# A buffer exchange in the first stage and new orders for the first and the last stage of a hybrid trunk kernel

## The chip, the cores and the metric

The kernel runs on one core of a Trainium2 chip. The metric is the device time of one execution in microseconds (us); lower is better. The profile calls the engines PE (TensorE, the matrix products; PEld is its weight load), DVE (VectorE), ACT (ScalarE), POOL (GpSimd) and SP (SyncE, which here only issues DMAs). [...]

## The reference

Two layers run over 512 latent tokens and 256 context tokens of width 1024. Each sub-layer is normed, shifted and scaled by a modulation of the conditioning vector, and its output is normed, gated and added to the residual stream:

```python
sh1, sc1, gt1, sh2, sc2, gt2 = ada_terms(c[:, None, :], w_mod[layer], b_mod[layer])
a = modulate(rms_norm(h, g_mix_pre[layer]), sh1, sc1)
...
y, yc = hybrid_mixer(a, ac, ...)      # layer 0: gated DeltaNet heads and attention heads
y = conformer_conv(a, *conf)          # layer 1
h = h + gt1 * rms_norm(y, g_mix_post[layer])
f = swiglu_ffn(modulate(rms_norm(h, g_ffn_pre[layer]), sh2, sc2), w_ffn_in[layer], w_ffn_out[layer])
h = h + gt2 * rms_norm(f, g_ffn_post[layer])
```

The context tokens enter layer 0 only, where they feed keys, values and the states of the DeltaNet heads. `conformer_conv` is a projection with a gate, a depthwise convolution over 31 tokens, a layer norm and a projection. `swiglu_ffn` is a gated product through 2816 hidden channels. Everything is float32.

## The kernel before, in words

A float32 product is made of three products of split operands: high by high, low by high and high by low, where `whi` is the rounded weight, `wlo` the remainder, and `ah`, `al` the same for activations. So nearly every product comes as three matmuls in turn, and every weight block of 128 x 1024 (512 KB, tile `wraw`) has first to be cast (`whi`, L564) and subtracted (`wlo`, L573).

The work goes in four stages. In each, operations are entered in a list by `op(...)`, with the engines that may do them and a cost on each, and class `Plan` then places them one at a time. Where an operation can go to two engines, the plan picks one. What is placed next is the operation with the smallest

```python
key = start - self.weight * lead, i
```

where `lead` is the length of the path behind the operation plus a number from a table `BIAS`, one per name of operation. The four tables are constants of the file. The plan runs when the kernel is built; on the chip each engine runs its own fixed list and waits by semaphore for data and buffers. A buffer pool is a `slot` in the plan (`take`, `rel`) and a tile with as many `bufs` in the code.

**First stage (`plan_inputs`, table `BIAS0`, 0 to 57 us).** Six token tiles of 128 x 1024 (four latent, two context; tile `xt`, three buffers) are loaded (`ld_x`, L351), squared and summed on ACT (`x_sq`, L355), get their root on DVE and POOL (L358, L180), are scaled in place on ACT or DVE (`x_norm`, L365 or L367), turned on PE in two halves of four transposes (`x_turn`, L374) and copied out of PSUM on ACT or DVE (`x_copy`, L314). Beside this sixteen modulation blocks of 512 KB (`mraw`, six buffers, `ld_m`, L404) are multiplied by the conditioning vector on PE (`mods`, L411). Two blocks make one group j of 128 channels: their rows are copied, turned on PE (`turn`, L426) and made into columns (L430, L431), and with these `mod` (L446, L448) shifts and scales the turned tokens, `a_high` rounds and `a_low` (L454) subtracts. The key and value products (`kv`, L297 to L299) follow, group by group. The PSUM banks of the turned tokens are those of the key and value products, so the latter begin when all six tiles are turned and copied out.

**Heads, and delta rule with attention (57 to 217 us and 217 to 392 us).** These two stages have tables of their own.

**Last stage (`BIAS2`, 392 to 1376 us).** The output projection, the first FFN, the conformer and the second FFN. `out_proj` makes token tiles t by halves n of the channels: matmuls into `ps_y` (L1760 to L1762), sum of squares on ACT (L1781), gate on DVE (`yg`, L1785), then root on POOL, residual on DVE (`hres`, L1810). The next sub-layer then norms (`xm`, L570), turns on PE (`ps_a`, L1832), and splits into `ah` and `al`. The gate, shift and scale rows of later sub-layers are made on DVE by 80 products with blocks `wada` of 512 KB (L1627), spread over the stage. The conformer convolves as a product in a transformed domain: its activations `ul`/`uh` go through PE (`ps_ft`), DVE and POOL form `spa`, `spb`, these are split (`sph`, `spl`, L573), and PE brings them back (`ps_y`, L2285 to L2287).

SP issues every load in the order that the plan wrote; an issue that waits for a buffer holds up all behind it.

Of the kernel before, what the change touches and what calls it, by code (L numbers as in the profile page):

```python
# [151 lines left out]
def kernel(ctx: ExitStack, tc: tile.TileContext, I: dict, out: bass.AP, dbg=None):  # L152
# [149 lines left out]
    with ExitStack() as st:  # L302
# [15 lines left out]
        def plan_inputs(op):  # L318
            last = {}
# [26 lines left out]
            def row_tile(t):  # L346
                s = {}

                def ld_x():
                    s["x"] = sp.tile([P, D], F32, tag="xt", name="xt", bufs=3)  # L350
                    SP.dma_start(s["x"], I["xs"][t * P : (t + 1) * P, :] if t < 4 else I["ctx"][(t - 4) * P : (t - 3) * P, :])  # L351

                def x_sq():
# [2201 lines left out]
```

## Time and profile before

| | us |
|---|---|
| median of 3 runs | 1379.72 (1378.24 to 1382.68) |
| the profiled execution, its own time | 1377.72 |
| its span, first to last instruction | 1375.9 |
| PE busy in the span | 1326.7 |
| mean granted clock of PE | 0.992 |

The profiled execution is 1.8 us longer than its span. A row of a timeline names an engine, a line of the kernel and what was written from what; the bracket behind it is the time for which the engine stood idle before it, and what released it. Rows that run back to back are drawn together with their count. The products of `mods` and `turn` are recorded as two matmuls each where the program has one, so eight records are one modulation block; eight transposes are one token tile.

### The profile page before, as it was taken

What the parts mean: (1) busy time and instruction counts of PE and PEld (TensorE: products, weight loads), DVE (VectorE), ACT (ScalarE), POOL (GpSimd) and SP (SyncE); (2) the same over time, 40 slices, a digit from 0 to 9 for tenths busy, and PEclk for the clock granted to TensorE, in tenths of its full rate; (3) what the DMA queues carried; (4) which work ended last, traced back from release to release, by engine and by line L of the source; (5) the groups of instructions that cost most, each with busy time, mean ns of one, the idle gap of its engine ahead of it and who ended that gap; (6) DMA issues with size and microseconds to landing.
All of it is one profiled execution on the core that took longest, in us unless ns stands there. A gap on an engine that the chain in (4) does not pass through costs nothing.

```text
span 1375.9 us, 19258 instructions
## 1 busy us (share of the span) xinstructions
PE 1326.7 (96%) x7343; PEld 1116.3 (81%) x7343; DVE 857.8 (62%) x1625; ACT 453.4 (33%) x983; POOL 256.7 (19%) x347
## 2 busy tenths in 40 slices
PE   5999898999999999999999999999999999999998
PEld 4888797898877888888887878887798888888886
DVE  3588897888888666565667476649663334243223
ACT  6656534877524301111000142114342223222221
POOL 2668563411002300000000011323040000000000
PEclk9999998999999999999999999999999999999999
DMA  8445636641157464545557333201113223233231
GB/s 320 136 147 165 157 116 148 218 143 55 38 203 262 158 200 150 185 160 177 184 202 256 117 103 103 73 28 62 61 65 120 92 92 110 74 122 108 93 105 64
DMA packets 105900, 184.76 MB, mean 134 GB/s; under 512 B 33776, under 2 KB 50496, under 8 KB 105808
## 3 DMA queue, kind: packets, MB, share of 16 engines
q1 hardware_dynamic: 105808, 183.53, 41.3%
q8 instruction: 58, 0.95, 0.3%
q14 instruction: 34, 0.28, 0.1%
HBM read 172.45 MB, written 11.06 MB: 133 GB/s over the span
## 4 chain that ended last, share of the span: by engine, by line
PE 74%; DVE 12%; DMA 7%; issue 2%; ACT 2%; POOL 2%; SPq 1%; DVEq 0%; POOLq 0%; ACTq 0%
PE ps_in L204 12%; PE ps_in L206 12%; PE ps_in L205 12%; PE ps_y L1760 5%; PE ps_y L1762 5%; PE ps_y L1761 5%; DMA wada<-in_wmB 3%; PE ps_in L2114 2%; PE ps_in L2112 2%; PE ps_in L2113 2%; DVE wlo L573 2%; PE ps_pt L1271 2%; DVE cv L653 2%; DVE wada L1627 1%; PE ps_pv L1293 1%
## 5 line engine op out<-in xcount | busy, mean ns | idle before, releaser
L205 PE MATMUL ps_in<-al,whi 128*128 128x512 f32 (+1 forms) x768 | 285.7, 372 | 1.6 <-POOL al L573 1.6
L206 PE MATMUL ps_in<-ah,wlo 128*128 128x512 f32 (+1 forms) x768 | 285.5, 372 | 0.8 <-DVE wlo L573 0.8
L204 PE MATMUL ps_in<-ah,whi 128*128 128x512 f32 (+1 forms) x768 | 285.9, 372 | 0.0
L573 DVE TENSOR_TENSOR wlo<-wraw,whi 128x1024 fp32r<-128x1024 f32 x162 | 204.7, 1265 | 116.4 <-ACT whi L564 109.2
L204 PEld LDWEIGHTS ps_in<-ah,whi 128*128 128x128 f32 x768 | 144.6, 188 | 28.1 <-issue 2.3
L205 PEld LDWEIGHTS ps_in<-al,whi 128*128 128x128 f32 x768 | 144.6, 188 | 27.3 <-POOL al L573 2.3
L206 PEld LDWEIGHTS ps_in<-ah,wlo 128*128 128x128 f32 x768 | 144.6, 188 | 26.7 <-DVE wlo L573 2.1
L180 POOL TENSOR_TENSOR rr<-rr,mhalf 128x1 f32<-128x1 f32 x28 | 17.4, 624 | 790.6 <-DVE rr L1799 765.0
L564 DVE CAST whi<-wraw 128x1024 fp32r<-128x1024 f32 x93 | 64.8, 697 | 158.0 <-PE ps_in L205 108.6
L1760 PE MATMUL ps_y<-whi,hh 128*128 128x512 f32 x352 | 138.0, 392 | 1.8 <-DVE yg L1785 1.8
L1762 PE MATMUL ps_y<-wlo,hh 128*128 128x512 f32 x352 | 137.7, 391 | 0.0
L1761 PE MATMUL ps_y<-whi,hl 128*128 128x512 f32 x352 | 137.6, 391 | 0.0
L1965 ACT ACTIVATE sg<-ps_in 128x512 f32<-128x512 f32 x44 | 26.3, 598 | 302.9 <-PE ps_in L206 302.6
L564 ACT CAST whi<-wraw 128x1024 fp32r<-128x1024 f32 x69 | 72.3, 1049 | 122.7 <-PE ps_y L1761 70.5
L1627 DVE CUSTOM_DVE_ANT_0 wada<-wada,csrow 128x1024 f32<-128x1024 f32 x80 | 97.3, 1231 | 19.7 <-DMA wada<-in_wmB 19.4
L1760 PEld LDWEIGHTS ps_y<-whi,hh 128*128 128x128 f32 x352 | 66.2, 188 | 16.5 <-DVE yg L1785 2.2
L1762 PEld LDWEIGHTS ps_y<-wlo,hh 128*128 128x128 f32 x352 | 66.2, 188 | 14.5
L1761 PEld LDWEIGHTS ps_y<-whi,hl 128*128 128x128 f32 x352 | 66.2, 188 | 14.3
L1781 ACT ACTIVATE junk<-ps_y 128x512 bf16<-128x512 f32 x32 | 19.1, 598 | 137.5 <-PE ps_y L1762 121.0
L1968 DVE TENSOR_TENSOR sg<-sg,ps_in 128x512 f32<-128x512 f32 x44 | 29.1, 682 | 45.5 <-PE ps_in L206 45.5
L653 DVE SCALAR_TENSOR_TENSOR cv<-ps_in,convw,cv 128x510 f32<-128x510 f32 (+3 forms) x80 | 48.9, 639 | 2.6 <-ACT cv L568 1.1
L2112 PE MATMUL ps_in<-whi,ah 128*128 128x512 f32 x128 | 50.0, 391 | 0.0
(390 smaller groups left out, 2584.0 us busy)
## 6 DMA issues: line engine op xcount, KB each, us to landing
wraw<-in_wfin SPq DMA_DIRECT2D x88, 512.0 KB
wada<-in_wmB SPq DMA_DIRECT2D x80, 512.0 KB
wraw<-in_wfout SPq DMA_DIRECT2D x44, 512.0 KB
mraw<-in_wmA SPq DMA_DIRECT2D x16, 512.0 KB
wraw<-in_wcin SPq DMA_DIRECT2D x16, 512.0 KB
wraw<-in_wqkv SPq DMA_DIRECT2D x12, 512.0 KB
wraw<-in_wcout SPq DMA_DIRECT2D x8, 512.0 KB
rw<-grow SPq DMA_DIRECT2D x8, 384.0 KB
```

Of the source, the lines that this page charges most:

```text
L204: E.matmul(ps, wh, xh, start=start, stop=False)
L205: E.matmul(ps, wh, xl, start=False, stop=False)
L206: E.matmul(ps, wl, xh, start=False, stop=stop)
L564: {"ACT": S.copy, "DVE": V.tensor_copy, "Pool": G.tensor_copy}[e](dst, src)
L573: {"DVE": V, "Pool": G}[e].tensor_tensor(dst, a, b, o)
L653: V.scalar_tensor_tensor(s["cv"][:, o], s["ps"][:, i], convw[:, ft, j : j + 1], s["cv"][:, o], op0=ALU.mult, op1=ALU.add)
L1627: V.tensor_tensor_reduce(s["raw"], s["raw"], csrow[0], 1.0, 0.0, ALU.mult, ALU.add, accs[:, part, j : j + 1])
L1760: E.matmul(acc[t], ah[:, ts_], wh[:, o], start=i == 0 and j == 0, stop=False)
L1761: E.matmul(acc[t], al[:, ts_], wh[:, o], start=False, stop=False)
L1762: E.matmul(acc[t], ah[:, ts_], wl[:, o], start=False, stop=end)
L1968: V.tensor_tensor(s["g"], s["g"], pss[1]["ps"], ALU.mult)
L2112: E.matmul(acc[t], k["h"][:, tk], wh[:, o], start=False, stop=False)
```

## The change

Two tables get new numbers: `BIAS0` and `BIAS2`. The buffers of the first stage are exchanged: five token tiles instead of three, four modulation blocks instead of six. In the plan's reckoning the first token load is given a longer way to its first user. The tables of the other two stages stay, and their PE, DVE, ACT and POOL orders are the same as before.

```diff
-BIAS0, TW0 = {'a_high': 75700, 'a_low': 206192, 'c_silu': -16514,
...
+BIAS0, TW0 = {'a_high': 4187, 'a_low': 281059, 'c_silu': 232311,
...
-BIAS2, TW2 = {'a_dot': -8768, 'a_dot1': -7091, 'a_dot3': -1746,
...
+BIAS2, TW2 = {'a_dot': -6282, 'a_dot1': -450, 'a_dot3': 2428,
...
-                    s["x"] = sp.tile([P, D], F32, tag="xt", name="xt", bufs=3)
+                    s["x"] = sp.tile([P, D], F32, tag="xt", name="xt", bufs=5)
...
-                a = last["x"] = op({"SP": 1.47}, ld_x, seq=after("x"), lat=DLAT, take=("xt",))
+                a = last["x"] = op({"SP": 1.47}, ld_x, seq=after("x"), lat=DLAT if "x" in last else DLAT + 2, take=("xt",))
...
-                        w["raw"] = sp.tile([P, 1024], F32, tag="mraw", name="mraw", bufs=6)
+                        w["raw"] = sp.tile([P, 1024], F32, tag="mraw", name="mraw", bufs=4)
...
-        plan = Plan({"a": 6, "r": 2, "xt": 3, "mraw": 6, "wraw": 2, "w": 4, "rows": 2, "a32": 2, "wkr": 2}, BIAS0, TW0, SCALE0)
+        plan = Plan({"a": 6, "r": 2, "xt": 5, "mraw": 4, "wraw": 2, "w": 4, "rows": 2, "a32": 2, "wkr": 2}, BIAS0, TW0, SCALE0)
```

The first place is PE from the first instruction to the first key and value product. Before (`x24` are three token tiles of eight transposes, `x4` of L411 one modulation block, L426 the turn of one group):

```order
L374 MATMUL ps_xt<-masks,xt 128x128 x24
L411 MATMUL ps_mod<-mraw,cz 32x256 x12
L426 MATMUL ps_mod<-quart,rows 128x2 x2
L374 MATMUL ps_xt<-masks,xt 128x128 x12
L411 MATMUL ps_mod<-mraw,cz 32x256 x4
L374 MATMUL ps_xt<-masks,xt 128x128 x4
L426 MATMUL ps_mod<-quart,rows 128x2 x2
L374 MATMUL ps_xt<-masks,xt 128x128 x8
L411 MATMUL ps_mod<-mraw,cz 32x256 x8
```

After, the same engine from the first instruction (behind these rows come the sixth token tile in two halves, a block behind each half, and a third turn, and then the first L297):

```order
L374 MATMUL ps_xt<-masks,xt 128x128 x8
L411 MATMUL ps_mod<-mraw,cz 32x256 x4
L374 MATMUL ps_xt<-masks,xt 128x128 x8
L411 MATMUL ps_mod<-mraw,cz 32x256 x4
L374 MATMUL ps_xt<-masks,xt 128x128 x8
L411 MATMUL ps_mod<-mraw,cz 32x256 x4
L374 MATMUL ps_xt<-masks,xt 128x128 x8
L426 MATMUL ps_mod<-quart,rows 128x2 x2
L411 MATMUL ps_mod<-mraw,cz 32x256 x4
L374 MATMUL ps_xt<-masks,xt 128x128 x8
L426 MATMUL ps_mod<-quart,rows 128x2 x2
L411 MATMUL ps_mod<-mraw,cz 32x256 x4
```

Blocks and turns now stand between single token tiles, and before the first key and value product there are seven blocks and three turns where there were six and two. On SP the first loads are now four latent tiles and one context tile, then three modulation blocks, then the last context tile; on ACT all six `x_norm` stand (L365), between the squares, and of the twelve `x_copy` eleven are on DVE.

The second place is DVE where the first half of the first FFN's output projection ends (`yg` takes it out of PSUM, the rows L1627 are products with `wada` blocks). Before:

```order
L573 TENSOR_TENSOR wlo<-wraw,whi 128x1024
L1627 ISA wada,accs<-wada,csrow 128x1024
L1627 ISA accs 128x1
L1627 ISA wada,accs<-wada,csrow 128x1024
L1627 ISA accs 128x1
L564 CAST whi<-wraw 128x1024
L573 TENSOR_TENSOR wlo<-wraw,whi 128x1024
L1627 ISA wada,accs<-wada,csrow 128x1024
L1627 ISA accs 128x1
L1785 TENSOR_TENSOR yg<-ps_y,gm 128x512 x3
```

After:

```order
L573 TENSOR_TENSOR wlo<-wraw,whi 128x1024
L564 CAST whi<-wraw 128x1024
L573 TENSOR_TENSOR wlo<-wraw,whi 128x1024
L564 CAST whi<-wraw 128x1024
L573 TENSOR_TENSOR wlo<-wraw,whi 128x1024
L1785 TENSOR_TENSOR yg<-ps_y,gm 128x512 x3
L564 CAST whi<-wraw 128x1024
```

The `wada` products of this part now stand further ahead, in the FFN's first half, and `yg` follows a weight split directly.

The third place is POOL in the last part of the conformer (`wlo` is the split of a whole weight block, `spl` that of the transformed activations). Before:

```order
L573 TENSOR_TENSOR ul<-csg,uh 128x256
L573 TENSOR_TENSOR spa<-spa,spd 128x512
L573 TENSOR_TENSOR spb<-spb,spc 128x512
L573 TENSOR_TENSOR wlo<-wraw,whi 128x1024 x2
L573 TENSOR_TENSOR spl<-spa,sph 128x512
L180 TENSOR_TENSOR mv<-mv,mhalf 128x1 x2
L573 TENSOR_TENSOR ul<-csg,uh 128x256
L573 TENSOR_TENSOR wlo<-wraw,whi 128x1024
L180 TENSOR_TENSOR mv<-mv,mhalf 128x1 x2
```

After:

```order
L573 TENSOR_TENSOR ul<-csg,uh 128x256
L573 TENSOR_TENSOR wlo<-wraw,whi 128x1024
L573 TENSOR_TENSOR spa<-spa,spd 128x512
L573 TENSOR_TENSOR spb<-spb,spc 128x512
L573 TENSOR_TENSOR wlo<-wraw,whi 128x1024 x2
L573 TENSOR_TENSOR ul<-csg,uh 128x256 x7
L573 TENSOR_TENSOR wlo<-wraw,whi 128x1024
L573 TENSOR_TENSOR ul<-csg,uh 128x256
L180 TENSOR_TENSOR mv<-mv,mhalf 128x1 x2
L573 TENSOR_TENSOR wlo<-wraw,whi 128x1024 x2
```

`spl` is gone from POOL, all twelve are on DVE now, and POOL has three `wlo` more in this piece; from the last tiles of the first FFN's output projection (820 us) to the end it has eight where it had five. In the out-projection around 430 us the transposes of the second token tile (L1832) stand six matmuls later on PE than before, and DVE has two `wada` products fewer ahead of the tile's `xm`.

## Rows read from the trace of the kernel before

**Rows 1.** Waits of PE, 0 to 57 us: total us, times, longest us.

```profile
PE ps_xt L374 <- DVE ssq_in L358: 12.4, 2, 10.9
```

**Rows 2.** Timeline of PE, 10 to 29 us: start, length, engine, line, work, [idle <-releaser].

```profile
10.92 4.63 PE L374 MATMUL ps_xt<-masks,xt 128*128 128x128 f32 x24 [10.92 <-DVE ssq_in L358]
15.48 1.50 PE L411 MATMUL ps_mod<-mraw,cz 128*32 128x256 f32 x24
17.10 0.61 PE L426 MATMUL ps_mod<-quart,rows 128*128 128x2 f32 x4
...
28.88 0.39 PE L297 MATMUL ps_kv<-wkhi,aL 128*128 128x272 f32 x1
```

**Rows 3.** Stretches: length, busy of PE, PEld, DVE, ACT, POOL, granted clock, DMA share, GB/s.

```profile
12.00:14.00 2.00, 2.00 (x12) 2.00 (x11) 1.48 (x4) 0.81 (x2) 0.55 (x1) 1.00 0.43 125
18.00:20.00 2.00, 0.55 (x5) 0.58 (x6) 0.98 (x2) 0.88 (x1) 0.51 (x1) 1.00 0.96 309
22.00:24.00 2.00, 1.98 (x12) 0.91 (x12) 1.29 (x2) 1.94 (x5) 0.92 (x2) 0.50 1.01 413
28.88:56.80 27.92, 27.92 (x253) 23.21 (x250) 10.56 (x30) 19.63 (x38) 15.30 (x15) 1.00 0.59 210
229.70:243.30 13.60, 12.60 (x92) 10.50 (x93) 7.74 (x20) 3.84 (x16) 2.86 (x10) 0.50 0.46 128
```

**Rows 4.** Timeline of the SP queue, 2 to 16 us.

```profile
2.59 1.38 SPq L351 DMA_DIRECT2D xt<-in_xs  x3
...
12.92 0.33 SPq L351 DMA_DIRECT2D xt<-in_xs  x1
```

**Rows 5.** Groups, 0 to 57 us: line, work, count, busy us, mean ns, idle.

```profile
L454 POOL TENSOR_TENSOR aL<-a,aL 128x512 fp32r<-128x512 f32 x8 | 10.4, 1296 | 11.0 <-ACT aL L314 10.9
...
L355 ACT ACTIVATE sq<-xt 128x1024 bf16<-128x1024 f32 x6 | 6.3, 1057 | 7.8 <-DMA xt<-in_xs 6.0 <-DMA xt<-in_ctx 1.6
...
L367 DVE TENSOR_SCALAR xt<-xt,ssq_in 128x1024 f32<-128x1024 f32 x6 | 4.5, 752 | 2.4 <-POOL ssq_in L180 2.3
```

**Rows 6.** Timeline of ACT, 8 to 10 and 21 to 25 us.

```profile
8.11 1.06 ACT L355 ACTIVATE sq<-xt 128x1024 bf16<-128x1024 f32 x1 [5.54 <-DMA xt<-in_xs]
9.07 0.19 ACT L355 ACTIVATION_READ_ACCUMULATOR sq<-xt 128x1 f32 x1
...
21.49 0.57 ACT L314 COPY xnT<-ps_xt 128x512 f32<-128x512 f32 x1
...
22.94 0.62 ACT L314 CAST aL<-a 128x512 fp32r<-128x512 f32 x1
...
23.94 1.10 ACT L338 CAST wkhi<-wkr 128x1088 fp32r<-128x1088 f32 x1
```

**Rows 7.** Waits of PE, 392 to 1376 us.

```profile
PE ps_a L1832 <- DVE xm L570: 3.1, 3, 1.7
...
PE ps_y L1760 <- DVE yg L1785: 1.8, 1, 1.8
...
PE ps_y L2286 <- DVE spl L573: 1.4, 1, 1.4
PE ps_y L1760 <- DVE ah L564: 1.2, 1, 1.2
```

**Rows 8.** Timeline of PE at 430 us.

```profile
430.69 1.06 PE L1832 MATMUL ps_a<-masks,xm 128*128 128x128 f32 x8 [1.12 <-DVE xm L570]
```

**Rows 9.** Timeline of DVE, 753 to 757 us.

```profile
753.58 1.23 DVE L1627 CUSTOM_DVE_ANT_0 wada<-wada,csrow 128x1024 f32<-128x1024 f32 x1
...
754.74 1.88 DVE L1785 TENSOR_TENSOR yg<-ps_y,gm 128x512 f32<-128x512 f32 x3
```

**Rows 10.** Timeline of DVE, 930 to 934 us.

```profile
930.22 0.68 DVE L573 TENSOR_TENSOR spl<-spa,sph 128x512 fp32r<-128x512 f32 x1
...
931.27 2.78 DVE L573 TENSOR_TENSOR spl<-spa,sph 128x512 fp32r<-128x512 f32 x1
```

**Rows 11.** Timeline of POOL, 931 us.

```profile
930.97 2.53 POOL L573 TENSOR_TENSOR wlo<-wraw,whi 128x1024 fp32r<-128x1024 f32 x1 [0.78 <-ACT whi L564]
```

More of the change, by code (lines that the diff above doesn't have):

```diff
@@ L132 @@
 XORD = (0, 1, 2, 3, 4, 5)
-BIAS0, TW0 = {'a_high': 75700, 'a_low': 206192, 'c_silu': -16514, 'c_tanh': 107271, 'col': 14441, 'e_ba': 122312, 'e_k': -53254, 'e_v': 50987, 'kv': -3858, 'ld_c': 46560, 'ld_k': -23712, 'ld_late': 35862, 'ld_m': -23721, 'ld_w': -44965, 'ld_x': -23461, 'mod': -8614, 'mods': 34406, 'quarters': 63428, 'rows': -16997, 'turn': -2462, 'w_high': 99939, 'w_low': 28294, 'x_copy': -10948, 'x_eps': 223488, 'x_norm': 166269, 'x_root': -3445, 'x_sq': 28280, 'x_turn': -3427, ('a_high', 'ACT'): 107926, ('a_high', 'DVE'): -198559, ('a_low', 'DVE'): 25709, ('a_low', 'Pool'): 56700, ('e_ba', 'ACT'): 44340, ('e_ba', 'DVE'): 44577, ('e_k', 'ACT'): 58673, ('e_k', 'DVE'): 49378, ('e_v', 'ACT'): -173612, ('e_v', 'DVE'): -10933, ('mod', 'ACT'): 3301, ('mod', 'DVE'): -9021, ('rows', 'ACT'): -15795, ('rows', 'DVE'): 40653, ('w_low', 'DVE'): 128023, ('w_low', 'Pool'): 46775, ('x_copy', 'ACT'): 9199, ('x_copy', 'DVE'): 8932, ('x_norm', 'ACT'): -81145, ('x_norm', 'DVE'): 61895}, 0.000200
+BIAS0, TW0 = {'a_high': 4187, 'a_low': 281059, 'c_silu': 232311, 'c_tanh': 40826, 'col': 135122, 'e_ba': 126776, 'e_k': 155419, 'e_v': 228586, 'kv': -6027, 'ld_c': 85019, 'ld_k': -25467, 'ld_late': 33477, 'ld_m': -25475, 'ld_w': 11636, 'ld_x': -23852, 'mod': -40306, 'mods': 118753, 'quarters': 54203, 'rows': 81455, 'turn': -4629, 'w_high': 15179, 'w_low': -332635, 'x_copy': 85335, 'x_eps': 366451, 'x_norm': 27921, 'x_root': 1752, 'x_sq': 107381, 'x_turn': -5686, ('a_high', 'ACT'): 92650, ('a_high', 'DVE'): -546573, ('a_low', 'DVE'): 58817, ('a_low', 'Pool'): 146574, ('e_ba', 'ACT'): 62505, ('e_ba', 'DVE'): 63100, ('e_k', 'ACT'): 129098, ('e_k', 'DVE'): 46060, ('e_v', 'ACT'): -269350, ('e_v', 'DVE'): 12404, ('mod', 'ACT'): 25634, ('mod', 'DVE'): 33866, ('rows', 'ACT'): -100952, ('rows', 'DVE'): 250644, ('w_low', 'DVE'): 430085, ('w_low', 'Pool'): -182664, ('x_copy', 'ACT'): 3255, ('x_copy', 'DVE'): 8749, ('x_norm', 'ACT'): 180579, ('x_norm', 'DVE'): -196162}, 0.000200
@@ new lines @@
+BIAS2, TW2 = {'a_dot': -6282, 'a_dot1': -450, 'a_dot3': 2428, 'a_end': 45182, 'a_end1': 27038, 'a_end3': 6873, 'b_high2': -58633, 'b_low2': 29028, 'b_sel2': -13825, 'c_comb2': -25178, 'c_high2': 125362, 'c_low2': -4724, 'c_open2': 18314, 'c_prod2': 58271, 'c_sig2': 68975, 'c_stat2': 28892, 'c_tok2': 136341, 'c_u2': 463, 'dft2': 54461, 'dft_q2': 52342, 'f_hi2': 33389, 'f_high1': 16934, 'f_high3': -62569, 'f_lo2': 12893, 'f_low1': 33751, 'f_low3': 41869, 'f_mult1': 134913, 'f_mult3': 9578, 'f_silu1': 45895, 'f_silu3': 63658, 'g_out': 23829, 'g_out1': -20936, 'g_out3': -28337, 'idft2': -172, 'idft_q2': -1472, 'ld_a': 73451, 'ld_a1': -8751, 'ld_a3': 209823, 'ld_b2': 41420, 'ld_f2': 71483, 'ld_g0': 27200, 'ld_g1': 93269, 'ld_g2': -9319, 'ld_g3': -29463, 'ld_h0': 7435, 'ld_s2': 1589, 'ld_w0': 18625, 'ld_w1': -2304, 'ld_w2': 69622, 'ld_w3': -14691, 'm_eps1': -5278, 'm_eps2': 8332, 'm_eps3': 7671, 'm_root1': 21497, 'm_root2': -11897, 'm_root3': 70059, 'm_sq1': -13259, 'm_sq2': -7014, 'm_sq3': 119678, 'm_x1': 11013, 'm_x2': -29310, 'm_x3': -5834, 'mm_in1': -279, 'mm_in3': 94, 'mm_q2': -1314, 'n_aggr2': 14267, 'n_root2': -722, 'n_x2': 108371, 'p_high1': 95748, 'p_high2': 34429, 'p_high3': -10939, 'p_low1': 30784, 'p_low2': 90184, 'p_low3': 15409, 'put1': -15738, 'put2': -2282, 'put3': 68953, 'q_comb2': -4970, 'q_cross2': 5014, 'q_hi2': 59756, 'q_lo2': 6027, 'q_prod2': 1128, 'reopen0': -80626, 'reopen1': -27164, 'reopen2': -32064, 's_mm2': -425, 's_put2': 72757, 'sp_hi2': 86991, 'sp_lo2': 59371, 'turn1': 11545, 'turn2': -271, 'turn3': 372, 'w_high0': 37508, 'w_high1': -159, 'w_high2': 2700, 'w_high3': 12123, 'w_low0': -32633, 'w_low1': 6514, 'w_low2': -5308, 'w_low3': 2305, 'y0': 871, 'y1': -4195, 'y2': -1584, 'y3': -118928, 'y_gate0': -2595, 'y_gate1': 30797, 'y_gate2': 1623, 'y_gate3': 15631, 'y_out3': -5278, 'y_res0': 8425, 'y_res1': -2763, 'y_res2': -1630, 'y_res3': -54137, 'y_root0': -8057, 'y_root1': 69924, 'y_root2': 41319, 'y_root3': -20071, 'y_sq0': -11883, 'y_sq1': -6243, 'y_sq2': 132, 'y_sq3': -36116, 'y_sum0': 37525, 'y_sum1': 52651, 'y_sum2': 23826, 'y_sum3': 97639, ('c_comb2', 'DVE'): -93901, ('c_comb2', 'Pool'): 34957, ('c_high2', 'ACT'): -116703, ('c_high2', 'DVE'): -2104, ('c_low2', 'DVE'): -14694, ('c_low2', 'Pool'): -13796, ('c_tok2', 'ACT'): 164820, ('c_tok2', 'DVE'): -24244, ('f_hi2', 'ACT'): -81770, ('f_hi2', 'DVE'): -51553, ('f_high1', 'ACT'): 84539, ('f_high1', 'DVE'): -71245, ('f_high3', 'ACT'): 45880, ('f_high3', 'DVE'): 44098, ('f_lo2', 'DVE'): 16554, ('f_lo2', 'Pool'): 21600, ('m_x1', 'ACT'): -50339, ('m_x1', 'DVE'): 54699, ('m_x2', 'ACT'): 51663, ('m_x2', 'DVE'): 72006, ('m_x3', 'ACT'): -12006, ('m_x3', 'DVE'): 6349, ('p_high1', 'ACT'): 18569, ('p_high1', 'DVE'): 9342, ('p_high2', 'ACT'): -40127, ('p_high2', 'DVE'): 5353, ('p_high3', 'ACT'): 14702, ('p_high3', 'DVE'): -137240, ('p_low1', 'DVE'): -34721, ('p_low1', 'Pool'): 12765, ('p_low2', 'DVE'): 120412, ('p_low2', 'Pool'): 69480, ('p_low3', 'DVE'): -57419, ('p_low3', 'Pool'): 62538, ('put1', 'ACT'): -7630, ('put1', 'DVE'): -74386, ('put2', 'ACT'): -7911, ('put2', 'DVE'): -6482, ('put3', 'ACT'): 27983, ('put3', 'DVE'): 70173, ('q_hi2', 'ACT'): 92517, ('q_hi2', 'DVE'): 80834, ('q_lo2', 'DVE'): -2487, ('q_lo2', 'Pool'): -29951, ('s_put2', 'ACT'): 112996, ('s_put2', 'DVE'): 37610, ('sp_hi2', 'ACT'): -24786, ('sp_hi2', 'DVE'): -7550, ('sp_lo2', 'DVE'): 103951, ('sp_lo2', 'Pool'): -77334, ('w_high0', 'ACT'): -88042, ('w_high0', 'DVE'): -33645, ('w_high1', 'ACT'): -105124, ('w_high1', 'DVE'): 4279, ('w_high2', 'ACT'): -10100, ('w_high2', 'DVE'): -8635, ('w_high3', 'ACT'): -2195, ('w_high3', 'DVE'): -7036, ('w_low0', 'DVE'): 172190, ('w_low0', 'Pool'): -126486, ('w_low2', 'DVE'): -614, ('w_low2', 'Pool'): -19785}, 0.000200
```

1 line of the change is left out of this document (removed).

## The prediction

> **What bounds the kernel now.** I read the waits of PE first, stage by stage, since PE is busy for 1326.7 of the 1375.9 us of the span. In the first stage the waits are long and few: 12.4 us for the roots of the token tiles, 10.9 of them before the first transpose [rows 1]. The timeline of PE shows the rest of the picture: three tiles turned in one run from 10.92 us, three modulation blocks, a turn, and then a thin stretch until the first key and value product at 28.88 [rows 2]. From there to 56.80 PE is busy for 27.92 of 27.92 us [rows 3], so what is gained before 28.88, or taken out of what lies behind it, moves the end of the stage by as much. The stretches tell why the middle is thin: DMA moves 125 GB/s in 12 to 14 us against 413 in 22 to 24, PE is busy for 0.55 of 2 us in 18 to 20, and afterwards its granted clock is 0.50 [rows 3]. SP shows the cause: three token loads go out at 2.59, and the fourth only at 12.92, when a token buffer is free [rows 4].
>
> In the last stage PE seldom waits. Its list of waits [rows 7] names DVE nearly throughout, and I followed three of them back: the one at 430.69 (1.12 us) [rows 8], the 1.8 us for `yg`, and the 1.4 us for `spl`. The two middle stages keep their orders and only shift.
>
> **First stage.** Before, the start of the key and value products hung on PE and the late loads. After, five token loads go out at once, so I expect the DMA gap to close and ACT to become what is late, because it gets the six scalings as well as the six squares. One square is 1.06 us on ACT with 0.19 to read its sum [rows 6]. A scaling of this size on ACT does not stand in the trace; from below I bound it by the same on DVE, 0.75, from above by two copies of half a tile on ACT, 0.57 each, 1.14 [rows 5, 6]. I take 1.06, the square of the same shape on the same engine. Six of each, 6 x (1.06 + 0.19 + 1.06) = 13.9 us, start at 8.11 as now and end at 22.0. The last scaling waits for its own root: before, the first turn starts at 10.92, which is 1.0 us more than 9.17 (end of the first square) plus 0.75 (scaling on DVE), and that is DVE and POOL. So 23.0. Then ACT casts the key weights, 1.10, and copies, shifts and rounds the first group, which before took from 21.49 to 23.56, 2.1 us; POOL subtracts, 1.30 [rows 5, 6]. Sum 27.5, and with 0.3 of handing over 27.8. DVE takes eleven of twelve copies out of PSUM, but it gives up six scalings and is busy for only about 1.3 of 2 us here [rows 3], so it is not late. The start comes 1.1 us earlier.
>
> Behind the start one block and one turn fewer are left, since seven and three are done where it was six and two: 1.50 / 3 = 0.50 and 0.61 [rows 2], another 1.1 us. The first stage so gives 2.2 us. From the good side: if ACT waits for nothing and the scalings cost 0.75, the start is at 24.6 by the same sum, bounded by PE itself, and I stop at 4 us in all. From the bad side: the four modulation buffers. A freed buffer is wanted again three blocks later. In the key and value part PE takes ten blocks in 27.92 us, 2.8 each, so 8.4 us; before it, seven blocks in some 14 us, so 6 us. A load takes up to 5.5 us (issued at 2.59, the first square at 8.11) [rows 4, 6]. That covers it by 0.5 us in the worse part; if a load takes 1 us longer there, three blocks are late by about that much each and the start is at 30 or so, which turns the gain into a loss of 1 to 2 us. So the term is -2.2, with ends -4 and +2.
>
> The low clock at 22 to 24 us goes with the thin stretch ahead of it. In the new order 14.6 us of PE work (six tiles at 4.63 / 3 = 1.54, seven blocks, three turns) lie between about 12 and 27.8, evenly, so I expect the clock to stay up. It pays little, since ACT is what is late then.
>
> **Last stage.** At 430.69 the transposes wait 1.12 us for `xm` [rows 8]. They now stand six matmuls later (six of 0.23 us, 1.4) and DVE has two `wada` products of 1.23 [rows 9] fewer ahead. The wait goes: -1.1, ends -1.1 and 0. What is late next is the same tile's split, and its matmuls stand behind the other out-projection work.
>
> At 755 PE waits 1.8 us for the banks that `yg` empties [rows 7]. DVE reads `wada` at 753.58 for 1.23 us and comes to `yg` at 754.74 [rows 9]. After, no such product stands in front of it; `yg` goes right behind a weight split. The wait goes: -1.8, ends -1.8 and 0. The 80 `wada` products are as many as before; they move into the first half of the FFN, where four for two blocks of matmuls leave DVE under three quarters busy by my count, so I cost them at nothing. If that cover fails, a weight is split late by one product, 1.2 us.
>
> The other waits of the list (`al` near 450, `xm` at 825, `spl` and `ah` in the conformer) I cost at no change. PE's order is rewritten around them, and each is a matter of tenths in a list that I can walk only with durations of the old order. Bounds: the 1.4 and 1.2 us of `spl` and `ah` and the rest of `xm`, 2.0, gone, -4.6; or the loss that the third rival prices.
>
> Sum: -2.2 - 1.1 - 1.8 = -5.1 us, from 1377.72 of the profiled execution to 1372.6. The median of the runs lies 2.0 us above the profiled execution, and I carry that over: 1374.6.
>
> **The rivals.** First, **the waits come back**. The tail's waits are set by small slips of DVE and POOL; one taken at 430 or 755 may be paid at the next `xm` or `al`. For it: at 430 a wait of the same kind follows within 25 us. Against it: at 755 the cause is a single instruction in the wrong place. Then only the first stage remains: 1379.72 - 2.2 = 1377.5.
>
> Second, **more waits go**: the conformer is rewritten most, and with 4.6 us there at stake, half of it gives 1372.3, all of it 1370.0.
>
> Third, on the other side, **POOL blocks DVE**. The subtraction `spl` of 128x512 takes 0.68 us on DVE, and 2.78 when it starts at 931.27, while POOL subtracts a whole weight from 930.97 on for 2.53 us [rows 10, 11]; both end within 0.6 us of each other. That is 2.1 us lost, of which 1.4 reach PE [rows 7]. From 820 us to the end POOL has five such `wlo` before, and three of PE's waits there (1.7, 1.4 and 1.2, together 4.3 us) follow one; after, it has eight, and all `spl` are on DVE. If all eight hit at 1.45 us, the waits are 11.6, 7.3 more than now: 1374.6 + 7.3 = 1381.9; if each costs PE the whole 2.1, 16.8, 12.5 more: 1387.1. It outweighs the 5.1 us of gains once four hits come on top of the three of before (4 x 1.45 = 5.8). Against it: the order may put the eight where DVE reads PSUM, and only three of five hit now.
>
> [...]
>
> Fourth, **the clock**. From 229.70 to 243.30 PE runs at 0.50 and is busy for 12.60 of 13.60 us [rows 3]. That stretch comes behind thin PE work that is not changed but shifts by 2 us. At full clock half of the 12.60, 6.3 us, would be saved: 1368.3; a second such stretch would cost as much: 1380.9. [...]
>
> **How the numbers follow.** 0.3%, 4.1 us, is about what a measurement of this kernel can tell from no change: below 1375.6 is faster, above 1383.9 slower. The forecast holds 0.45, with a range of its own of 1371 to 1378, two thirds of it on the faster side (0.30 faster, 0.15 same). The waits that come back: 0.20 (0.03 faster, 0.17 same). More waits go: 0.12, faster. POOL blocks DVE: 0.15 (0.12 slower, 0.03 same). The clock: 0.08 (0.04, 0.02, 0.02). Together faster 0.49, same 0.37, slower 0.14. The range of 8 in 10 takes in the first two whole, most of the third and the lower half of POOL: 1368 to 1382.
>
> **What would show it.** Right: the fourth token load on SP before 5 us, no stretch at 0.50 between 18 and 29 us, the first key and value product near 27.8 and the stage's last near 54.6 (56.8 before); no wait of `yg` near 755 and none of `xm` over 0.5 at 430. Wrong: waits of `mods` for a block of over 0.5 us in the first stage, ACT's last scaling later than 24, a new wait over 1 us behind `xm`, `al` or `spl` in the last stage, or DVE subtractions of over 2 us beside POOL's `wlo` in the conformer with PE waiting for them.

## The result and the profile after

The changed kernel takes 1382.81 us in the median of 20 runs (1375.99 to 1385.09), the kernel before 1377.95 in the median of 20 (1371.0 to 1382.68). The ratio is 1.0035, 95% interval 1.0025 to 1.0045: slower by some 4.9 us, where 5.1 us faster was forecast. The profiled execution after has this span and mean granted clock (1.00 is the full one):

```profile
core 0: 1381.2 us, clock 0.990
```

That is 5.3 us more than the 1375.9 of before. The table gives the length of each part in the two profiled executions, from the first matmul of the part to the first of the next, read from PE's timeline (the conformer from its first product with a weight, L2112; the second FFN to the start of its last matmul):

| part | before | after |
|---|---|---|
| first stage, to the first product of the heads | 56.6 | 54.2 |
| heads, delta rule and attention | 335.9 | 335.6 |
| output projection and turn, to the first product of the first FFN | 49.8 | 51.7 |
| first FFN, first half | 250.8 | 252.1 |
| first FFN, output projection | 125.0 | 124.9 |
| conformer | 186.8 | 191.6 |
| second FFN | 364.4 | 364.1 |

In this pair of executions the first stage gained what was forecast, and the last stage lost three times that, most of it in the conformer. The stretches further down show how much of the pair's difference goes with the clock.

**The first stage.** Waits of PE in 0 to 57 us after (before: [rows 1]):

```profile
PE ps_xt L374 <- ACT xt L365: 11.4, 1, 11.4
PE ps_mod L411 <- DMA mraw<-in_wmA: 1.0, 1, 1.0
```

In place of the 12.4 us for the roots stand one wait of 11.4 us at the start and 1.0 us for the first modulation block. PE's timeline, rows that answer to [rows 2]:

```profile
11.40 1.97 PE L374 MATMUL ps_xt<-masks,xt 128*128 128x128 f32 x8 [11.40 <-ACT xt L365]
14.35 1.08 PE L411 MATMUL ps_mod<-mraw,cz 128*32 128x256 f32 x8 [0.98 <-DMA mraw<-in_wmA]
...
27.01 0.37 PE L297 MATMUL ps_kv<-wkhi,aL 128*128 128x272 f32 x1
```

The first key and value product comes at 27.01 us, 1.9 earlier than before. On the SP queue ([rows 4] before):

```profile
2.59 1.85 SPq L351 DMA_DIRECT2D xt<-in_xs  x4
4.49 1.50 SPq L351 DMA_DIRECT2D xt<-in_ctx  x1
```

Five token loads are out before 6 us. ACT's timeline, to set beside [rows 6]:

```profile
7.83 1.06 ACT L355 ACTIVATE sq<-xt 128x1024 bf16<-128x1024 f32 x1 [5.11 <-DMA xt<-in_xs]
...
10.21 1.13 ACT L365 ACTIVATE xt<-xt,ssq_in 128x1024 f32<-128x1024 f32 x1
...
21.44 1.15 ACT L365 ACTIVATE xt<-xt,ssq_in 128x1024 f32<-128x1024 f32 x1 [1.78 <-POOL ssq_in L180]
...
24.81 0.62 ACT L314 CAST aL<-a 128x512 fp32r<-128x512 f32 x1
```

A scaling takes 1.13 us on ACT, the last one starts at 21.44, and the first group is rounded at 24.81. The stretches of the kernel after (columns as in [rows 3]: length, busy of PE, PEld, DVE, ACT, POOL, clock, DMA share, GB/s):

```profile
12.00:14.00 2.00, 1.36 (x7) 0.96 (x5) 0.15 (x1) 2.00 (x4) 0.55 (x1) 1.00 1.01 406
18.00:20.00 2.00, 2.00 (x16) 1.51 (x16) 1.42 (x3) 1.66 (x3) 0.00 (x0) 1.00 1.02 415
22.00:24.00 2.00, 2.00 (x28) 1.51 (x20) 1.96 (x6) 2.00 (x4) 0.00 (x0) 1.00 0.87 274
...
227.80:241.40 13.60, 13.57 (x98) 11.14 (x99) 8.12 (x19) 4.81 (x16) 3.54 (x9) 0.51 0.46 121
391.80:398.80 7.00, 6.63 (x17) 5.27 (x18) 6.90 (x9) 0.00 (x0) 0.00 (x0) 0.54 0.66 202
954.30:957.80 3.50, 3.50 (x20) 3.40 (x18) 3.50 (x15) 1.86 (x4) 0.00 (x0) 0.54 0.47 154
```

DMA moves 406 GB/s in 12 to 14 us where it moved 125, PE is full in 18 to 20, and the clock at 22 to 24 is 1.00 where it was 0.50. The last three rows show the other side: the half-clock stretch of the delta stage is there as before, and there are two more, within the windows 391.8 to 398.8 and 954.3 to 957.8 (6.8 and 3.4 us at half clock, so worth up to 3.4 and 1.7 us, half of each: before, eight transposes took 1.95 us from 25.67 on, at clock 0.50, and 1.06 from 19.45 on, at 1.00).

**The last stage.** Waits of PE after 392 us (before: [rows 7]):

```profile
PE ps_a L1832 <- DVE xtok L2350: 3.9, 2, 2.0
PE ps_y L1762 <- DVE wlo L573: 3.0, 4, 1.6
PE ps_a L1832 <- DVE xm L570: 2.9, 3, 1.5
PE ps_y L2286 <- DVE spl L573: 2.1, 3, 1.1
PE ps_in L206 <- DVE wlo L573: 1.3, 2, 0.8
PE ps_y L1760 <- DVE whi L564: 0.7, 1, 0.7
...
```

The waits for `yg` and `ah` are gone. In their place stand 3.9 us for `xtok`, the conformer's tokens after the layer norm, a name that the list of before had at 0.3 us. `spl` went from 1.4 to 2.1. The waits for splits of weights grew as well: `wlo` at L1762 from 2.3 to 3.0, `wlo` at L206 from 0.8 to 1.3, and 0.7 for `whi` at L1760, which is new. The `xtok` wait on three engines, DVE, POOL and PE, in this order:

```profile
947.68 6.03 DVE L2350 TENSOR_SCALAR xtok<-xtok,mv 128x512 f32<-128x512 f32 x4
```

```profile
948.59 4.82 POOL L573 TENSOR_TENSOR wlo<-wraw,whi 128x1024 fp32r<-128x1024 f32 x2
```

```profile
951.27 0.66 PE L1832 MATMUL ps_a<-masks,xtok 128*128 128x128 f32 x4 [2.03 <-DVE xtok L2350]
953.76 0.87 PE L1832 MATMUL ps_a<-masks,xtok 128*128 128x128 f32 x6 [1.83 <-DVE xtok L2350]
```

Four scalings of 128x512 on DVE take 6.03 us. The first two take 0.54 us each; the third starts at 948.75 and takes 2.47, the fourth 2.56, while POOL subtracts two whole weights from 948.59 to 953.41. PE waits twice, and then runs at half clock (the 954.3 row above). The same between `spl` on DVE and a `wlo` on POOL, on the first `wlo` of the POOL piece that was shown as the third place of the change:

```profile
883.22 2.77 DVE L573 TENSOR_TENSOR spl<-spa,sph 128x512 fp32r<-128x512 f32 x1
```

```profile
882.87 2.57 POOL L573 TENSOR_TENSOR wlo<-wraw,whi 128x1024 fp32r<-128x1024 f32 x1
```

2.77 us where it is 0.69 undisturbed, and it ends 0.55 us after POOL does.

### The profile page after: what moved, and what is told of

Same layout as the page of the kernel before. It is cut to its first block, busy times and chain, and to the rows that moved or that the text cites. A ratio compares the mean times of both kernels' runs of the same rounds, so it can differ in the third digit from the quotient of the medians.

```text
span 1381.2 us, 19311 instructions
## 1 busy us (share of the span) xinstructions
PE 1331.7 (96%) x7343; PEld 1116.9 (81%) x7343; DVE 869.2 (63%) x1635; ACT 446.5 (32%) x967; POOL 266.3 (19%) x353
## 4 chain that ended last, share of the span: by engine, by line
PE 62%; DVE 17%; DMA 12%; ACT 3%; issue 2%; POOL 2%; SPq 1%; DVEq 0%; POOLq 0%; ACTq 0%
PE ps_in L206 7%; PE ps_in L204 7%; PE ps_in L205 7%; PE ps_y L1762 6%; PE ps_y L1760 6%; PE ps_y L1761 6%; DMA wada<-in_wmB 5%; DMA wraw<-in_wfin 4%; DVE wlo L573 4%; DVE wada L1627 3%; DVE whi L564 2%; PE ps_in L2112 2%; PE ps_in L2114 2%; PE ps_in L2113 2%; PE ps_pt L1271 2%
## 5 line engine op out<-in xcount | busy, mean ns | idle before, releaser
L206 PE MATMUL ps_in<-ah,wlo 128*128 128x512 f32 (+1 forms) x768 | 286.1, 373 | 1.9 <-DVE wlo L573 1.3
L573 DVE TENSOR_TENSOR wlo<-wraw,whi 128x1024 fp32r<-128x1024 f32 x159 | 198.7, 1251 | 113.8 <-ACT whi L564 106.8
L206 PEld LDWEIGHTS ps_in<-ah,wlo 128*128 128x128 f32 x768 | 144.6, 188 | 29.3 <-DVE wlo L573 4.4
L1760 PE MATMUL ps_y<-whi,hh 128*128 128x512 f32 x352 | 138.1, 392 | 0.7 <-DVE whi L564 0.7
L1762 PE MATMUL ps_y<-wlo,hh 128*128 128x512 f32 x352 | 137.8, 392 | 0.6 <-DVE wlo L573 0.6
L1627 DVE CUSTOM_DVE_ANT_0 wada<-wada,csrow 128x1024 f32<-128x1024 f32 x80 | 97.5, 1234 | 49.5 <-DMA wada<-in_wmB 49.5
L1760 PEld LDWEIGHTS ps_y<-whi,hh 128*128 128x128 f32 x352 | 66.1, 188 | 16.0 <-DVE whi L564 1.1
L1762 PEld LDWEIGHTS ps_y<-wlo,hh 128*128 128x128 f32 x352 | 66.2, 188 | 15.5 <-DVE wlo L573 1.0
L573 POOL TENSOR_TENSOR matsl<-fraw,matsh 128x512 fp32r<-128x512 f32 x5 | 8.1, 1644 | 319.4 <-ACT matsh L564 319.4
L573 POOL TENSOR_TENSOR wlo<-wraw,whi 128x1024 fp32r<-128x1024 f32 x22 | 54.1, 2460 | 47.6 <-DVE whi L564 25.4
```

Source lines behind the costliest of these rows:

```text
L206: E.matmul(ps, wl, xh, start=False, stop=stop)
L573: {"DVE": V, "Pool": G}[e].tensor_tensor(dst, a, b, o)
L1627: V.tensor_tensor_reduce(s["raw"], s["raw"], csrow[0], 1.0, 0.0, ALU.mult, ALU.add, accs[:, part, j : j + 1])
L1760: E.matmul(acc[t], ah[:, ts_], wh[:, o], start=i == 0 and j == 0, stop=False)
L1762: E.matmul(acc[t], ah[:, ts_], wl[:, o], start=False, stop=end)
```

## The experiments

Two theories stood after the result. **A:** the first stage gains some 2 us, and the last stage's new order loses more than it saves, mainly since POOL's whole-weight subtractions in the conformer hold DVE instructions that PE waits for. **Rival:** the first stage's shift costs, through the clock, or the DVE rows are late by their own order. Ratios are to the kernel before, measured beside it, each with its 95% interval; the number of executions is 6 to 12 for each kernel, and one where it says so.

**The two halves of the change alone.** First the new first stage with the old table for the last:

```diff
-BIAS2, TW2 = {'a_dot': -6282, ...   (table after)
+BIAS2, TW2 = {'a_dot': -8768, ...   (table before)
```

> The change with the last stage's table of before: only the first stage is changed. Theory A (the first stage gains 2.6 us, the last stage loses it and more): 2.6 us under before, ratio about 0.998, first key and value product near 27, out-projection from 389.9 us, then a last stage as long as before. Rival (the earlier start alone sets the clock back, as the half-clock stretch at 391 to 398 us in the profile of the changed kernel would say if it comes from the shift): the gain is lost again there, ratio 1.000, with the granted clock 0.50 for some 7 us behind 391.

Measured: 0.9989 (0.9971 to 1.0007), 1376.41 us. The first stage ends at 53.8 us, the conformer takes 186.7. The gain is 1.5 us in the times, for 2.6 expected, with an interval that takes in no change, and 2.8 us of the first stage in the profile. The rival, that the shift alone brings the half clock at 391, is not borne out: the order up to 392 us is that of the changed kernel, and the same stretch has the full clock here, while a half-clock stretch stands at 755, behind a wait for `yg` of 2.2 us (windows of this kernel):

```profile
391.80:398.80 7.00, 7.00 (x32) 5.63 (x31) 3.65 (x6) 0.00 (x0) 0.00 (x0) 1.00 0.87 280
755.00:758.50 3.50, 3.50 (x10) 2.68 (x10) 2.33 (x5) 0.00 (x0) 0.00 (x0) 0.53 0.25 71
```

Then the old first stage with the new table for the last:

```diff
-BIAS2, TW2 = {'a_dot': -8768, ...   (table before)
+BIAS2, TW2 = {'a_dot': -6282, ...   (table after)
```

> Before with the last stage's new table and nothing else. Theory A: out-projection starts at 392.5 as before, the conformer is 4.8 us longer, the whole 5 to 7.5 us over before, ratio 1.0036 (no low clock behind 391) to 1.0055 (with it). Rival (the first stage's change is what costs, through the clock): ratio under 1.002.

Measured: 1.0038 (1.0021 to 1.0055), 1383.53 us; the conformer takes 191.7 us, the FFN's first half 254.6. The last stage's order carries the loss. This profile has 6.8 us at half clock behind its `xtok` waits, at 949.8, with the old first stage.

**Two subtractions off POOL.** The plan is left as it is; only where it hands the seventh and eighth of these splits to POOL, DVE does them:

```diff
-                tt_on(e, s["l"], s["raw"], f32(s["h"]), ALU.subtract)
+                tt_on("DVE" if e == "Pool" and (seen.append(1) or len(seen) in (7, 8)) else e, s["l"], s["raw"], f32(s["h"]), ALU.subtract)
```

> The changed kernel with its last two whole-weight subtractions of POOL (948.6 to 953.4 us) on DVE, where they stand behind the splits of the second pair of token tiles; every other engine's order as it was. Theory A (POOL's subtraction holds up DVE's xtok, 6.03 us for four, and PE waits 2.03 and 1.83 us and then runs at half clock): the four xtok take about 2 us, both waits are under 0.5, no low clock at 954 to 958; 4 to 5.5 us under the changed kernel, ratio to before about 1.000. Rival (xtok is late for the order on DVE, not for POOL): the waits stay and DVE has 2.5 us more to do; ratio 1.0035 or above.

Measured: 1.0003 (0.999 to 1.0016), 1379.15 us, 3.2 thousandths or 4.4 us under the changed kernel. The same four scalings on DVE:

```profile
948.51 2.07 DVE L2350 TENSOR_SCALAR xtok<-xtok,mv 128x512 f32<-128x512 f32 x4
```

2.07 us instead of 6.03. The waits of PE in 820 to 1010 us:

```profile
PE ps_y L2286 <- DVE spl L573: 2.3, 4, 1.1
PE ps_y L1762 <- DVE wlo L573: 1.8, 3, 1.0
PE ps_a L1832 <- DVE xm L570: 1.5, 1, 1.5
```

`xtok` is gone from the list, `wlo` has 1.0 us more (the two moved splits come a little late), and the clock stays at 1.00 in 942 to 970 us. The conformer takes 187.7 us, 3.9 less: PE's waits there are 2.8 us shorter, and the 3.4 us at half clock are gone. Theory A holds here, and the rival falls.

**All eight off POOL:**

```diff
-tt_on("DVE" if e == "Pool" and (seen.append(1) or len(seen) in (7, 8)) else e, ...
+tt_on("DVE" if e == "Pool" and (seen.append(1) or len(seen) in range(9)) else e, ...
```

> The changed kernel with all eight whole-weight subtractions that POOL has from 820 us on moved to DVE, at the place in the order where they were. Theory A: besides what the last two give (4 to 5.5 us) the waits for xm at 825.9 (1.50) and for spl at 882, 886 and 897 (0.62, 1.10, 0.36) go: up to 3.5 us more, ratio about 0.998. Rival (DVE becomes late: six more subtractions of 1.2 us on it, two of them right ahead of a split that PE waits for): new waits of about 1.2 us each at those places, ratio 1.000 or above the kernel with two moved.

Measured: 0.9982 (0.9963 to 1.0001), 1376.06 us; the conformer takes 185.7 us. The waits of PE in 820 to 1010:

```profile
PE ps_y L1762 <- DVE wlo L573: 2.3, 3, 1.5
PE ps_y L2286 <- DVE spl L573: 0.8, 2, 0.6
PE ps_in L2114 <- DVE wlo L573: 0.8, 1, 0.8
...
```

The waits for `xm` and two of the three for `spl` are gone; the wait of 0.62 for `spl` near 881 stays, so that one was never POOL's. So five of the eight subtractions had a wait of PE behind them. Waits for `wlo` of 0.8 and 1.5 us came in their place, as the rival said in part.

**The same edit in the kernel before**, where it moves five:

```diff
-tt_on(e, s["l"], s["raw"], f32(s["h"]), ALU.subtract)
+tt_on("DVE" if e == "Pool" and (seen.append(1) or len(seen) in range(9)) else e, ...
```

> Before with the five whole-weight subtractions that POOL has from 820 us on moved to DVE at their place in the order. Theory A (POOL's subtraction holds DVE for its whole length): the waits behind them (xm 1.72 at 825.6, spl 1.40 at 936.9, ah 1.23 at 952.1) go, up to 4.3 us; DVE has five times 1.2 us more, so some of it comes back as waits for a split: 2 to 4 us under before, ratio 0.997 to 0.9985. Rival (these waits are DVE's own lateness): no gain, ratio 1.000 to 1.003.

Measured: 0.9967 (0.9952 to 0.9983), 1373.93 us; the conformer takes 183.6 us, 3.2 less. Waits of PE in 820 to 1010:

```profile
PE ps_in L2114 <- DVE wlo L573: 0.8, 1, 0.8
PE ps_y L1762 <- DVE wlo L573: 0.7, 2, 0.4
PE ps_in L206 <- DVE rr L1876: 0.6, 1, 0.6
PE ps_y L2286 <- DVE spl L573: 0.3, 1, 0.3
...
```

None of the three waits that [rows 7] showed in this stretch is left. **With the new first stage as well** (the same edit on the kernel with the first stage alone):

> The new first stage with the last stage of before, and its five whole-weight subtractions of POOL on DVE: the sum of the first-stage kernel (ratio 0.9989) and of what moving five gives. If the two add up: 0.996 to 0.9975, some 4 to 5.5 us under before. If the first stage's gain is given back on the way to the last stage, the same as with the five alone.

Measured: 0.9956 (0.994 to 0.9972), 1372.15 us. This is the fastest version measured: the first stage of the change, the last stage of before, and no weight split on POOL from 820 us on. The two gains add within their intervals. Set beside the kernel with all eight moved (0.9982), which has the same first stage and no weight split on POOL either, it is 2.6 thousandths or 3.6 us faster, with intervals that just overlap. So POOL's subtractions are not the whole loss of the new last stage: taking them away gives 5.3 thousandths in the new order, but 3.3 in the old one too.

**POOL's work without its data.** In the kernel with two moved, POOL gets two subtractions at the old place whose result nobody reads:

```diff
                 def n_root(t=t):
                     rsqrt(r["r"][:, 1:2], r["r"][:, 1:2])
+                    for _ in range(2 if t == 1 else 0): G.tensor_tensor(spare, spare, spare, ALU.subtract)
```

> The changed kernel with its last two whole-weight subtractions on DVE (ratio 1.0003), and in their place on POOL two subtractions of 128x1024 on a spare tile that nobody reads. Theory A (it is POOL's work as such that holds DVE): the third and fourth xtok take about 2.5 us each again, PE waits about 2.0 and 1.8 us for them, and 3 to 5 us of the gain are gone, ratio 1.002 to 1.004. Rival (moving them helped since the data came from another engine or in another order): xtok stays at 0.54 us and the ratio at 1.0003.

Measured: 1.0027 (1.0011 to 1.0043), 1380.85 us. DVE, POOL, and PE's wait in 820 to 1010:

```profile
945.54 5.13 DVE L2353 TENSOR_SCALAR xtok<-xtok,mv 128x512 f32<-128x512 f32 x4
```

```profile
946.46 3.92 POOL L2345 TENSOR_TENSOR spare<-spare 128x1024 f32<-128x1024 f32 x2
```

```profile
PE ps_a L1834 <- DVE xtok L2353: 3.0, 2, 1.6
```

The four scalings take 5.13 us again (the third 2.02, the fourth 2.11), beside POOL rows of 1.89 and 1.96, and PE waits 3.0 us. It is POOL's work as such that holds DVE here, whatever becomes of its result. The time is that of the kernel with two moved plus 2.4 thousandths, 3.3 us, which agrees with the 3.0 of waits. The clock stays full behind these waits (1.00 in 948 to 958).

**The plan told to leave POOL out** in the conformer, and planned anew:

```diff
-s["op"] = op({"DVE": 1.14, "Pool": 2.31} if ph[0] in ("0", "2") else {"DVE": 1.14}, w_low, ...
+s["op"] = op({"DVE": 1.14, "Pool": 2.31} if ph[0] == "0" else {"DVE": 1.14}, w_low, ...
```

> The changed kernel with POOL taken from the ways of the weight split in the conformer before the order is planned, so that the whole last stage's order is planned anew with the changed tables. Theory A: no DVE row is held by a POOL subtraction of a weight; if the order that comes out is no worse, the ratio is that of the kernel with all eight moved by hand, 0.998. Rival (the table fits only the order it was searched for): new waits of DVE or of weights in the conformer, ratio above 1.000.

Measured: 1.0087 (1.0064 to 1.011), 1391.31 us; the conformer takes 199.4 us, with waits of 2.9, 2.3 and 4.4 us and 3.4 and 10.2 us at half clock behind them. The rival holds: with one way less, these numbers make an order that is worse than what POOL costs.

**The `wada` products of the first FFN.** On the kernel with all eight moved, `a_dot1` and `ld_a1` get their old numbers:

```diff
-'a_dot1': -450, ... 'ld_a1': -8751,
+'a_dot1': -7091, ... 'ld_a1': -12898,
```

> The changed kernel with all eight whole-weight subtractions on DVE (ratio 0.9982), and for the loads and products of wada in the first FFN the two old numbers of the table: two products per two channel groups in the FFN's first half where the changed kernel has four (before: three), the rest in its output projection. Theory B (the moved products make DVE late with the FFN's weight splits): the FFN's first half, 252.0 to 254.6 us with the changed order, comes back to 250.5 to 251.5; the yg wait may come back by 1 to 2 us in the output projection; together -2 to +1 us against 0.9982. Rival (the FFN's first half is longer for its order on PE): it stays at 252 or more.

Measured: 1.0144 (1.0116 to 1.0172), 1399.7 us. On the part it was made for theory B holds: the FFN's first half takes 250.0 us, where the six other kernels with the new last stage took 251.9 to 254.6 and the six with the old 250.8 to 251.7. PE's order in that half is the same as in the changed kernel; DVE has 26 `wada` products there, for 48 in the changed kernel and 36 before. On the whole the expectation failed by far, since the products went to the end of the FFN and PE waited there (440 to 850 us):

```profile
PE ps_a L1832 <- DVE xm L570: 8.9, 3, 5.2
PE ps_y L1760 <- DVE whi L564: 6.3, 1, 6.3
PE ps_in L2107 <- DVE sel L2031: 5.0, 1, 5.0
PE ps_in L206 <- DVE wlo L573: 0.7, 1, 0.7
```

Behind these waits PE ran at half clock for 10.2 us from 798.1 and for 20.5 us from 828.9, which is part of the loss.

**The first stage in its parts**, one execution each; both keep the longer way of the first token load. The new table with the old buffers (its three places drawn together):

```diff
-tag="xt", name="xt", bufs=5)   tag="mraw", name="mraw", bufs=4)   "xt": 5, "mraw": 4
+tag="xt", name="xt", bufs=3)   tag="mraw", name="mraw", bufs=6)   "xt": 3, "mraw": 6
```

> The first stage's new table with the old buffers (three token tiles, six modulation blocks); the last stage is that of before. Theory A (the fourth and fifth token buffer carry the gain): the fourth token load waits until 12 us or later as before, the stage ends at 56 us or later (before 56.5, with both 53.8 to 55.5). Rival (the new order carries it): it ends near 54.5.

Measured: the stage ends at 61.7 us, 5.0 later than before. The order puts a modulation block first, and PE's first instruction waits for it:

```profile
PE ps_mod L411 <- DMA mraw<-in_wmA: 13.3, 3, 12.0
```

The new buffers with the old table:

```diff
-BIAS0, TW0 = {'a_high': 4187, ...   (table after)
+BIAS0, TW0 = {'a_high': 75700, ...   (table before)
```

> The first stage's new buffers (five and four) with the old table; the last stage is that of before. Theory A: five token loads go out before 5 us, the first key and value product comes near 27 and the stage ends at 54 to 55.5. Rival (the order carries the gain): 56 us or later; all token tiles are turned before the first modulation block here, so the blocks may come late to their products.

Measured: the stage ends at 64.2 us. All six tiles are turned first, and the products of the blocks wait for an operand that DVE makes behind the scalings:

```profile
PE ps_mod L411 <- DVE cz L472: 3.1, 1, 3.1
```

Neither expectation holds. In these single executions each half alone makes the stage 5.0 and 7.6 us longer, and only the pair makes it shorter: nothing here says that the buffers or the order carry the gain.

## Why the prediction was wrong

Every sign that the prediction named for being right held in the profile after, and the kernel was slower all the same. Three of its signs for being wrong held as well: 1.0 us of waiting for a modulation block, a new wait of 1.1 us for `spl`, and DVE instructions of over 2 us beside POOL's `wlo` with PE waiting for them.

- **First stage, -2.2: right in sign, and near the mark by luck.** A scaling cost 1.13 us for the 1.06 taken, and the clock stayed up. But the sum had 1.1 us for an earlier start and 1.1 us for less work behind it, and both were off. Over the eight kernels with this stage the start of the key and value products is at 26.9 us in the mean, for 28.8 in the three with the old one: 1.9 us. The part behind it takes 28.1 us for 27.7: 0.4 more, not 1.1 less. The stage ends at 55.0 in the mean (53.8 to 56.3) for 56.5: 1.5 us. Nor did the start hang on ACT, as the sum had it: ACT's path, with POOL's first subtraction at its end, was done by 26.8, but in the profile after, the chain of work that ended last goes through the load of the first modulation block, and from 14.35 to 27.01 PE has no wait over 0.15 us:

```profile
6.03 8.18 DMA mraw<-in_wmA
```

  What is missing behind the start is the cover of the modulation buffers. I had a load at up to 5.5 us, taken from the first token load, and 8.4 us of cover, as if PE took the blocks evenly. In six of the eight kernels PE waits there for blocks, 0.6 to 1.8 us in all; in the best version (12 to 57 us):

```profile
PE ps_mod L411 <- DMA mraw<-in_wmA: 2.8, 4, 1.1
```

  Of the 2.8 us, 1.0 is the first block, at 14.2, and the rest, 1.8, is blocks at 29.6, 32.3 and 43.8. The load of the block at 32.3 took 8.10 us in this kernel's chain:

```profile
24.07 8.10 DMA mraw<-in_wmA
```

  In the profile shown above no wait for a later block is over 0.15 us, and the stage ends at 54.2.
- **430 us, -1.1: not shown.** The wait is absent in the profile after, but in the kernel with two subtractions moved, which has the same order there, it is 1.80 at 429.9. In the kernels with the old last stage it is 1.06 to 1.94 or absent. It was no fixed price that an order takes away. The reason was off too: DVE has eight `wada` products ahead of this `xm` for nine, one fewer and not two, and it stood idle before `xm` both times, for the root that POOL makes (before, then after):

```profile
430.05 0.88 DVE L570 TENSOR_SCALAR xm<-hres,rr 128x512 f32<-128x512 f32 x2 [0.67 <-POOL rr L180]
```

```profile
429.70 0.88 DVE L570 TENSOR_SCALAR xm<-hres,rr 128x512 f32<-128x512 f32 x2 [0.67 <-POOL rr L180]
```

- **755 us, -1.8: the wait went, the time did not.** The first FFN's output projection takes 124.9 us for 125.0: waits for `whi` and `wlo` of 0.7 and 0.6 us near 717 stand in its place. In the six kernels with the old order the `yg` wait was 0.3 to 2.2 us, so part of the 1.83 was this one execution's. In the mean this part takes 124.3 us with either order, where no half-clock stretch falls in it.
- **The `wada` products "at nothing": wrong by some 1.5 us.** The count was right, DVE is busy for 174.0 of 252.1 us there, under three quarters, but such a share does not say that every split comes in time. The FFN's first half takes 252.9 us in the mean of six kernels with the new order, 251.4 in six with the old. The last experiment on it ties the loss to the products. The price that the prediction named for a failing cover was 1.2 us.
- **"The other waits ... I cost at no change": the step that failed.** The conformer lost 4.9 us (191.6 and 191.7 for 186.7 to 186.8 in four kernels with the order of before). In the two profiles PE's waits there go from 5.4 to 8.3 us, and 3.4 us at half clock come in behind the `xtok` waits. It is the third rival's mechanism, POOL's subtractions holding DVE, and 4.4 of the changed kernel's 4.9 us come back when two subtractions leave POOL. I counted eight `wlo` for five and then took the forecast's value from a list of waits of the old order, although the rows on either side of the new POOL rows could be read: in the order after, two `wlo` follow the root that releases `xtok`, and `xtok` is what PE turns next. I looked for `spl`, with two operands in SBUF. `xtok` has one, and was held about as long: 2.47 and 2.56 us for 0.54, where `spl` took 2.77 for 0.69.
- **The third rival's sum, 1381.9 to 1387.1, holds the measured 1382.81, and that is partly luck.** The rival had 0.15. Five of the eight subtractions hit, for 6.8 us of waits where three of five had 4.3: 2.5 us more, not 7.3. I had held against this rival that the eight may stand where DVE reads PSUM, and both profiles have such rows that were not held: `spa` from `ps_ft` takes 0.69 us at 870.06 before, beside POOL's `wlo` of 2.41 us from 869.05, and 0.69 at 939.65 after, beside the one of 3.27 us from 938.25, for 0.68 at 953.62 with POOL idle. The rest of the miss is the gains at 430 (not shown) and 755 (none in the mean), the `wada` products, and what the new order loses in the conformer without any weight split on POOL: 185.7 us, for 183.6 and 183.8 with the old order.
- **The clock rival: stretches came, but the changed kernel did not run at a lower clock as a whole.** Over all executions its mean granted clock was 0.991, and that of the kernel before, beside the experiments, 0.989, which takes in the stretch at 22 us that the new first stage does not have. With the old first stage and the new last one it was 0.988, so half clock can be a part of the last stage's loss, some 2 us by these means. In the profile, half-clock stretches appeared at 391.8 and 954.3. The second follows the `xtok` waits and went with them, but in the kernel with idle work on POOL the waits came back and the half clock did not. The first is not the order's: the kernels with two subtractions moved and with idle work on POOL have the same order there and the full clock. What sets such a stretch off, no run here shows; the rival's price is an estimate from the 12.60 us of the stretch at 229.70.
- **The 2.0 us from profile to median** were an accident of three runs; over 20 the median of before is 1377.95, beside the profile's 1377.72.

What stays open: from 390 to 440 us the new order takes 49.1 to 51.6 us and the old 49.6 to 50.7, where no half-clock stretch falls in it, so no gain or loss can be told there; why the new order is slower in the conformer even without weight splits on POOL (two waits of the kernel with all eight moved, 0.6 us for `spl` near 881 and 1.5 us for a moved `wlo` near 954, make up about as much) was not tried; and the spread in the middle stages (332 to 337 us with one and the same order, with half-clock stretches of 3 to 20 us) was not taken apart.

## What to carry to other kernels

Before a list of old waits is used as the price of a new order, read what each POOL row of the new order stands beside: a POOL subtraction of 2.4 us cost DVE more here than it saved it, and it cost the kernel time where the DVE row that it held fed PE, in five cases of eight. A split moved to POOL to relieve DVE saved 1.2 us of DVE's time and took 2 us from it. A table of such numbers belongs to its buffers and its ways: with half of the first stage's pair that stage was 5.0 and 7.6 us longer than before, and with one way less the conformer was 7.8 us longer than with it.

## What the hardware showed that I had not expected

Beside two POOL subtractions in a row, one DVE instruction passed for each: the third `xtok` ends 0.3 us behind POOL's first subtraction, the fourth 0.3 us behind the second, with POOL rows of 2.3 and 2.5 us as with those of 1.9 and 2.0. A scaling with one operand in SBUF is held about as long as a subtraction with two, 2.5 us beside 2.8. So is a cast: `sph` of 128x512 took 1.50 us at 892.80 and ended 0.3 us behind a POOL subtraction that had begun just before it, and 0.41 undisturbed. Half-clock stretches of 3 to 7 us came at waits of PE in one execution and not in another with the same instruction order (391.8 to 398.8 us: 0.54 after, 1.00 in the kernel with two subtractions moved, whose order is the same there).
